# Attention scores of two heads in one three-bank PSUM tile, sink column and inverse denominators on GpSimd

## Chip, cores, metric

The kernel runs on one core of one Trainium2 chip. The metric is the device time of one execution in microseconds (us). A core has five engines with instruction streams of their own: TensorE (PE in the profile; its weight loads are listed as PEld), VectorE (DVE), ScalarE (ACT), GpSimd (POOL) and SyncE (SP), which issues most DMAs here. Each runs its instructions in order and waits on semaphores for the others. SBUF holds tiles of 128 partitions; PSUM, which matmuls write, has 8 banks of 512 f32 values a partition.

## What is computed

Two layers over 1024 latent and 256 context tokens. Layer 0 mixes with a chunked gMLP, layer 1 with windowed attention; a ConvGLU follows each. The change lies in the attention of layer 1: 16 query heads, 4 key/value heads, one softmax over the latent keys at a distance of at most 128, all 256 context keys and a sink logit of the head.

```
def softmax_with_sink(logits, sink):
    sink_col = jnp.broadcast_to(...)
    p = jax.nn.softmax(jnp.concatenate([logits, sink_col], axis=-1), axis=-1)
    return p[..., :-1]
...
    def one_block(args):
        j, qj = args
        kj = lax.dynamic_slice_in_dim(kp, j * BLOCK, band, axis=1)
        ...
        s_lat = jnp.einsum('bqhgd,bkhd->bhgqk', qj, kj).astype(jnp.float32) * scale
        s_lat = jnp.where(valid, s_lat, -jnp.inf)
        s_ctx = jnp.einsum('bqhgd,bkhd->bhgqk', qj, kc).astype(jnp.float32) * scale
        p = softmax_with_sink(jnp.concatenate([s_lat, s_ctx], axis=-1), sink)
```

## The kernel before

All matmuls run on float32 values split into a high and a low part in fp32r: `S.copy` rounds the high part on ACT and `V.tensor_sub` makes the rest on DVE.

Attention runs over `pairs` (L1849): query block `j` of 128 rows (8 of them), key/value head `g` (4), and a pair `pr` of its four query heads (2), so 64 pairs. Block 0 and block 7 see two latent key tiles, the others three, and all see two context tiles; a row of scores has NK = 512 or 640 columns, and NL of them are latent. The loop at the end of the kernel function (`for i in range(n_pairs + LC)`) issues for each `i`: `q_prep` (transposes of the next queries, one PSUM bank), `att_a` of pair i, `att_b` of pair i - 2, `att_c` of pair i - 3, then steps of the output projection `o_steps`.

- `att_a`: the scores, in two forms. Pairs 8 to NM - 1 = 23 are *merged*: each head has a two-bank tile `psA` of its own, six matmuls fill it (256, 256 and 128 columns, high and low keys), and one DVE instruction (`tensor_tensor_reduce`, `CUSTOM_DVE_ANT_0` in the profile, `ISA` in the order) adds the mask, writes the row to SBUF and takes its extreme with the sink logit. Other pairs are *split*: both heads' latent scores lie in one `psA` tile, a bank a head, both heads' context scores in one `psB` bank, and each head takes two such instructions, of NL and of 256 columns, the second starting from the first's extreme. Scores have their sign turned, so the maximum is a minimum here.
- `softmax`: from block 2 on (`es is None`) the sink logit stands as one more column behind the row. DVE copies it there (`V.tensor_copy`), ACT takes the exponential with its sum, DVE inverts the sums (`V.reciprocal`) and POOL scales the two rows. In blocks 0 and 1 POOL adds the sink's term and inverts as a power of -1 with the constant `mone`.
- `att_b`: the rows are transposed in 128 x 128 pieces into `psB` tiles, and ACT and DVE make high and low parts (`act`).
- `att_c`: products with the values into a `psB` tile; ACT copies one half, DVE adds the halves to the block's row tile. After a block's last pair the row tile is split and stored to `oscr` in DRAM, one DMA on ACT's queue and one on SP's.
- `o_steps`: the output projection for blocks 0 and 1, 2 and 3, 4 and 5, each in two halves of eight steps. Each step loads weights (`wh` from `woscr`) and rows (`oc` from `oscr`), and adds six 512-column matmuls to a `psA` tile that is held for a half. They start at i = 20, 36 and 52 (`sched`). At the end of a half ACT copies the tile to `acc`, in the step that follows the last matmuls. Blocks 6 and 7 are projected behind the loop (`last_o`).

PSUM is one pool `ps` for the whole kernel: `psA` twice two banks, `psB` four times one. Tiles come from rings: a tile of a tag takes the place of the one `bufs` allocations earlier and waits until that one is no longer used. The wait of a matmul for a reader of the same tile is set by the recording layer, and that layer also decides the order on each engine: it starts from the program's order and puts ahead what its own estimates take to be ready. So the order on an engine is a result, and a change of one operation can move others.

Names in the profile: `psB<-act,y` are the products with the values, `psB<-ident,tmp` and `psB<-ident,wl` the transposes of the two heads' rows, `psA<-big,tmp` and `psB<-big,tmp` the scores (`big` are the keys, `tmp` the queries), `psA<-wh,oc` the projection, `act<-psB,act` DVE's hi/lo difference of `att_b`, `sm` the small statistics. A row of a group has the line of a helper, L50, for all of them.

Of the kernel before, what the change touches and what calls it, by code (L numbers as in the profile page):

```python
# [32 lines left out]
def hybrid_kernel(  # L33
# [37 lines left out]
    open_pool("mix")  # L71
    ps = ctx.enter_context(tc.tile_pool(name="ps", bufs=1, space=bass.MemoryType.PSUM))
    dr = ctx.enter_context(tc.tile_pool(name="dr", bufs=1, space=bass.MemoryType.DRAM))
# [56 lines left out]
    def psA(shape=(P, 2, 512)):  # L130
        return ps.tile(list(shape), F32, name=nm("psA"), tag="psA", bufs=2)

    def psB(shape=(P, 512)):
        return ps.tile(list(shape), F32, name=nm("psB"), tag="psB", bufs=4)

# [43 lines left out]
    ones = ones_r.bitcast(F32)  # L179
    mhalf = const.tile([P, 1], F32, name="mhalf")  # L180
    G.memset(mhalf, -0.5)
    mone = const.tile([P, 2], F32, name="mone")
    G.memset(mone, -1.0)
# [639 lines left out]
    def gmlp(si, hb, tiles, gate, extra, between, pre_last, on_flip=None, head=None, order=(0, 1, 2, 3, 4), mod=None):  # L823
        st = const.tile([P, 5, 24], F32, name=nm("st"))
        if head:
# [28 lines left out]
        rs, nmr = t_sm(5), t_sm(5)  # L854
        mv = t_sm(10).rearrange("p (i n) -> p i n", i=5)
        for i in range(5):
# [960 lines left out]
    def after_b(bi, u):  # L1817
# [9 lines left out]
        if bi == 2:  # L1827
# [5 lines left out]
            if u == 2:  # L1833
                q_prep(0, 1)

    maskw = const.tile([P, 640], F32, name="mask")
    G.memset(maskw, 0.0)
# [4 lines left out]
                    pattern=[[-1, 384]], channel_multiplier=1)  # L1842
    NM = 24
    snk = const.tile([P, NH], F32, name="snk")
# [5 lines left out]
    HEAD = 2  # L1850

    def softmax(Pt, mx, es, dn, h0, NK):
        if es is None:
            for h in range(2):
                S.activation(Pt[h][:, 0:NK + 1], Pt[h][:, 0:NK + 1], AF.Exp, bias=mx[:, h:h + 1], scale=-1.0,
                             accum_out=dn[:, h:h + 1])
            V.reciprocal(dn, dn)
            for h in range(2):
                G.tensor_scalar(out=Pt[h][:, 0:NK], in0=Pt[h][:, 0:NK], scalar1=dn[:, h:h + 1], scalar2=0.0,
                                op0=ALU.mult, op1=ALU.add)  # L1860
            return
        G.tensor_tensor(out=es, in0=snk[:, h0:h0 + 2], in1=mx[:, 0:2], op=ALU.add)
        for h in range(2):
            S.activation(Pt[h][:, 0:NK], Pt[h][:, 0:NK], AF.Exp, bias=mx[:, h:h + 1], scale=-1.0,
                         accum_out=dn[:, h:h + 1])
        S.activation(es, es, AF.Exp)
        G.tensor_tensor(out=dn, in0=dn, in1=es, op=ALU.add)
        G.tensor_tensor(out=dn, in0=dn, in1=mone, op=ALU.pow)
        for h in range(2):
            G.tensor_scalar(out=Pt[h][:, 0:NK], in0=Pt[h][:, 0:NK], scalar1=dn[:, h:h + 1], scalar2=0.0,  # L1870
                            op0=ALU.mult, op1=ALU.add)

    def merged(j, g, pr):
        return 8 <= 8 * j + 2 * g + pr < NM

    def att_a(j, g, pr):
        k0, kts = geo[j]
# [4 lines left out]
        mx, es, dn = t_sm(4), t_sm(2) if j < 2 else None, t_sm(2)  # L1882
        Pt = [t_tmp((P, 648)), t_w("wl", F32, (P, 648))]
        if es is None:
            for h in range(2):
                V.tensor_copy(Pt[h][:, NK:NK + 1], nsnk[:, h0 + h:h0 + h + 1])
        if merged(j, g, pr):
            for h in range(2):
                lh = qs[:, 2 * pr + h, :]
                sl = psA()  # L1890
                for dst, c in ((sl[:, 0, 0:256], 1024), (sl[:, 0, 256:512], k0 * P), (sl[:, 1, 0:P], k0 * P + 256)):
# [3 lines left out]
                V.tensor_tensor_reduce(out=Pt[h][:, 0:NK], in0=sl.rearrange("p a b -> p (a b)")[:, 0:NK],  # L1895
                                       in1=maskw[:, 0:NK], scale=1.0,
                                       scalar=nsnk[:, h0 + h:h0 + h + 1], op0=ALU.add, op1=ALU.min,
                                       accum_out=mx[:, h:h + 1])
# [25 lines left out]
    def att_b(j, g, pr):  # L1924
# [3 lines left out]
        for a in range(0, nk, 2):  # L1928
            n = min(2, nk - a)
            pt = psB((P, 2, 2, P))  # L1930
            for b in range(n):
                for h in range(2):
                    T.transpose(out=pt[:, b, h, :], in_=Pt[h][:, (a + b) * P:(a + b + 1) * P], identity=ident)
            S.copy(PTh[:, a:a + n], pt[:, 0:n])
# [5 lines left out]
    def att_c(j, g, pr):  # L1940
        kts = geo[j][1]
        nk = len(kts)
        if merged(j, g, pr):
            kts = kts[-2:] + kts[:-2]
# [25 lines left out]
    def o_steps(tiles):  # L1970
# [34 lines left out]
        for i in range(nt):  # L2005
# [51 lines left out]
    while next(og, 1) is None:  # L2057
        tick()

    def last_o():  # L2060
# [20 lines left out]
    lat_ffn(1, 3, 5, halos, gate_of(1, 5), chain(last_o(), flushes(True)), ada_steps(1, 5, (0,), True))  # L2081
    stage_pool["guard"].__exit__(None, None, None)


# [40 lines left out]
```

## Time and profile before

| | us |
|---|---|
| median of three runs | 2849.98 (2846.95 to 2852.19) |
| the profiled execution | 2852.14 |
| its span, first to last instruction | 2850.4 |
| attention loop, pairs 20 to 63 | about 1883 to 2130 |
| mean granted TensorE clock | 0.99 |

The page gives busy times over the span, groups of instructions and the chain of work that ended last; the trace answers for any stretch. A group's row reads: line, engine, operation, names out<-in, shape, count | busy us, mean ns of one | idle time of the engine just before, with what ended it. A row of waits reads: engine, what it was to write, what it waited for: total us, times, longest. A row of the timeline: start, length, engine, operation, count, and in brackets the idle time before it. A matmul is listed with its full passage, so matmuls that follow each other overlap in the list; how far their starts lie apart is what each costs PE.

### The profile page before, as it was taken

Reading aid. Unit: us, or ns where it says so; the run is one execution under the profiler, and the core shown is the slowest. Engines: PE = TensorE matmul, PEld = TensorE weight load, DVE = VectorE, ACT = ScalarE, POOL = GpSimd, SP = SyncE. Lnnn points to the kernel's source line nnn. Section 1 sums busy time; section 2 is a strip of 40 time slices with the busy share of each in tenths; the row PEclk is TensorE's granted clock in tenths of the full one; section 3 lists DMA queues with packets and bytes.
Section 4 is the critical chain, followed back from the end, with each engine's and each line's share of the span. In section 5 each row is a group of like instructions: output and inputs, shape, how many; then the busy total and the mean of one; then the engine's idle time right before and its main releaser. Section 6 shows DMA issues by size and latency. Waiting matters only on the chain.

```text
span 2850.4 us, 40321 instructions
## 1 busy us (share of the span) xinstructions
PE 2735.4 (96%) x14570; PEld 2348.8 (82%) x14570; DVE 2218.6 (78%) x3466; ACT 1390.8 (49%) x2291; POOL 623.2 (22%) x806
## 2 busy tenths in 40 slices
PE   7999999999989999999999999899998999999998
PEld 5798887898879888888888788788887888888886
DVE  6567685687779898887786658898887788888776
ACT  4233243232367444455444545777876444445433
POOL 1064021260110122121000124543332122220000
PEclk9999999999999999999999999999999999999999
DMA  7785447554478345467845665347577355445753
GB/s 261 237 244 171 146 142 240 184 158 127 174 233 249 121 159 170 143 219 231 313 157 187 201 210 188 115 139 238 186 241 231 122 168 179 157 144 196 254 176 125
DMA packets 436335, 537.13 MB, mean 188 GB/s; under 512 B 20004, under 2 KB 300452, under 8 KB 436135
## 3 DMA queue, kind: packets, MB, share of 16 engines
q1 hardware_dynamic: 379575, 470.84, 51.5%
q10 hardware_dynamic: 55408, 59.52, 6.2%
q0 software_dynamic: 1152, 4.19, 0.4%
q8 instruction: 115, 1.88, 0.3%
q14 instruction: 85, 0.70, 0.1%
HBM read 414.40 MB, written 120.07 MB: 188 GB/s over the span
## 4 chain that ended last, share of the span: by engine, by line
PE 69%; DVE 12%; DMA 9%; ACT 4%; issue 4%; POOL 2%; SPq 1%; ACTq 0%; DVEq 0%; POOLq 0%
PE psB L50 52%; PE psA L50 17%; DVE row L50 3%; DMA raw<-in_ada_w_dram 3%; DVE wl L50 3%; DVE acc L50 1%; DVE tmp L50 1%; ACT wh L50 1%; DVE y L50 1%; ACT tmp L50 1%; DMA raw<-in_f_w_up_dram 1%; DMA xT<-row 1%; SPq L50 1%; POOL sm L50 1%; DVE act L50 1%
## 5 line engine op out<-in xcount | busy, mean ns | idle before, releaser
L50 PE MATMUL psB<-cmb,wh 128*128 128x512 f32 (+2 forms) x2584 | 750.5, 374 | 8.1 <-ACT row L50 5.6
L50 PEld LDWEIGHTS psB<-cmb,wh 128*128 128x128 f32 x2584 | 471.9, 188 | 99.2 <-ACT row L50 8.0
L50 PE MATMUL psB<-cmb,wl 128*128 128x512 f32 (+2 forms) x1292 | 482.9, 374 | 0.0
L50 ACT CAST wh<-raw 128x1024 fp32r<-128x1024 f32 (+1 forms) x313 | 265.2, 863 | 436.4 <-PE psB L50 173.6
L50 DVE TENSOR_TENSOR wl<-raw,wh 128x1024 fp32r<-128x1024 f32 (+1 forms) x313 | 308.9, 1002 | 97.2 <-ACT wh L50 95.5
L50 PEld LDWEIGHTS psB<-cmb,wl 128*128 128x128 f32 x1292 | 243.1, 188 | 43.6 <-DVE wl L50 0.2
L50 PE MATMUL psB<-wh,big 128*128 128x512 f32 x816 | 271.4, 399 | 4.0 <-ACT big L50 1.3
L50 ACT CAST wh<-row 128x1024 fp32r<-128x1024 f32 (+1 forms) x196 | 162.5, 834 | 189.9 <-DVE row L50 97.0
L50 PE MATMUL psB<-wh,act 128*128 128x512 f32 x640 | 200.2, 391 | 0.8 <-DVE tmp L50 0.8
L50 POOL TENSOR_TENSOR row<-raw,raw 128x512 f32<-128x512 f32 x44 | 73.2, 1664 | 572.2 <-DMA raw<-in_f_w_up_dram 516.6
L50 PE MATMUL psA<-big,wh 128*128 128x320 f32 x1024 | 194.4, 312 | 0.3 <-ACT row L50 0.3
L50 DVE TENSOR_TENSOR wl<-row,wh 128x1024 fp32r<-128x1024 f32 (+1 forms) x196 | 185.4, 949 | 11.8 <-ACT wh L50 11.8
L50 DVE SCALAR_TENSOR_TENSOR acc<-raw,ccols,acc 128x1024 f32<-128x1024 f32 x98 | 125.8, 1302 | 81.2 <-DMA raw<-in_ada_w_dram 81.1
L50 PEld LDWEIGHTS psB<-wh,big 128*128 128x128 f32 x816 | 154.7, 191 | 40.2 <-ACT big L50 2.4
L50 DVE SCALAR_TENSOR_TENSOR row<-row,cwcols,row 128x1024 f32<-128x1024 f32 (+2 forms) x142 | 150.8, 1062 | 39.2 <-ACT row L50 22.6
L50 ACT CAST ah<-raw 128x1024 fp32r<-128x1024 f32 x80 | 77.6, 974 | 202.2 <-PE psB L50 80.9
L50 POOL TENSOR_SCALAR row<-row,sm,sm 128x128 f32<-128x128 f32 x160 | 146.0, 926 | 114.0 <-DMA row<-vscr 63.3
L50 DVE TENSOR_TENSOR row<-row,row 128x512 f32<-128x512 f32 (+4 forms) x169 | 156.9, 932 | 17.3 <-DMA row<-actd 10.5
L50 PEld LDWEIGHTS psA<-big,wh 128*128 128x128 f32 x1024 | 160.9, 189 | 0.7 <-ACT row L50 0.5
L50 PE MATMUL psB<-wl,big 128*128 128x512 f32 x408 | 157.9, 397 | 0.6 <-DVE wl L50 0.6
L50 DVE TENSOR_TENSOR al<-raw,ah 128x1024 fp32r<-128x1024 f32 x80 | 90.3, 1128 | 71.4 <-ACT ah L50 71.1
L50 PE MATMUL psB<-row,wh 128*128 128x256 f32 x744 | 133.6, 283 | 9.5 <-ACT wh L50 7.5
(279 smaller groups left out, 6210.7 us busy)
## 6 DMA issues: line engine op xcount, KB each, us to landing
raw<-in_f_w_up_dram SPq DMA_DIRECT2D x121, 512.0 KB, 4.9
raw<-in_ada_w_dram SPq DMA_DIRECT2D x88, 512.0 KB, 4.4
raw<-in_a_w_in_dram SPq DMA_DIRECT2D x64, 512.0 KB, 4.6
wh<-woscr SPq DMA_DIRECT2D x48, 512.0 KB, 4.4
row<-actd SPq DMA_DIRECT2D x44, 512.0 KB, 5.3
actc<-row SPq DMA_DIRECT2D x44, 512.0 KB, 4.1
raw<-actc SPq DMA_DIRECT2D x40, 512.0 KB, 3.8
actd<-row SPq DMA_DIRECT2D x39, 512.0 KB, 2.6
```

Of the source, the lines that this page charges most:

```text
L50: ins = fn(*a, **kw)
```

## The change

- PSUM becomes three pools, one after the other. The first is as before and ends ahead of pair NM, now 20. The second has one score tile `psS` of three banks, one projection tile `psO` of two and three `psB`. The third, as the first, opens behind the loop. They are opened so that a tile waits only for the tiles whose place it takes.
- From pair 20 on all pairs are *joined*: both heads' scores lie in the one `psS`, head 0's row over banks 0 and 1 (its latent columns end where its context columns begin), head 1's over banks 1 and 2. Each head has four matmuls and one DVE instruction for the whole row. Head 0 has its latent columns first, head 1 its context columns, which `att_b`, `att_c` and the mask (256 columns longer) follow. Pairs 20 to 23 were merged before, 24 to 63 split.
- From pair 16 on the rows of a pair are allocated while the pair before is at its scores, and POOL copies the sink's column into them then.
- From block 2 on POOL inverts the denominators, as it did in blocks 0 and 1.
- `o_steps` copies the finished half to `acc` in the step of its last matmuls.
- Small constants share tiles (`powers`, and the statistics of the gMLP), which pays for the longer mask.

```
+    def psS():
+        return banks_pool["pool"].tile([P, 1536], F32, name=nm("psS"), tag="psS", bufs=1)
+
+    def psO():
+        return banks_pool["pool"].tile([P, 2, 512], F32, name=nm("psO"), tag="psO", bufs=1)
...
-    NM = 24
+    NM = 20
...
-            V.reciprocal(dn, dn)
+            G.tensor_tensor(out=dn, in0=dn, in1=mone, op=ALU.pow)
...
-        Pt = [t_tmp((P, 648)), t_w("wl", F32, (P, 648))]
-        if es is None:
+        Pt = rows_of.pop((j, g, pr), None) or [t_tmp((P, 648)), t_w("wl", F32, (P, 648))]
+        nxt = 8 * j + 2 * g + pr + 1
+        if 16 <= nxt < len(pairs):
+            nj, ng, npr = pairs[nxt]
+            rows_of[nj, ng, npr] = [t_tmp((P, 648)), t_w("wl", F32, (P, 648))]
+            nk = len(geo[nj][1]) * P
             for h in range(2):
-                V.tensor_copy(Pt[h][:, NK:NK + 1], nsnk[:, h0 + h:h0 + h + 1])
+                G.tensor_copy(rows_of[nj, ng, npr][h][:, nk:nk + 1],
+                              nsnk[:, 4 * ng + 2 * npr + h:4 * ng + 2 * npr + h + 1])
...
+        if joined(j, g, pr):
+            sl = psS()
+            for h in range(2):
+                lh = qs[:, 2 * pr + h, :]
+                local, o = (512 - NL, 512 - NL) if h == 0 and j < 7 else (512 * h + 512, 512 * h + 256)
+                context = 512 if h == 0 and j < 7 else 512 * h + 256
+                for c, k, n in ((local, k0 * P, NL), (context, 1024, 256)):
+                    T.matmul(sl[:, c:c + n], lh, KH[g][:, k:k + n], start=True, stop=False)
+                    T.matmul(sl[:, c:c + n], lh, KL[g][:, k:k + n], start=False, stop=True)
+                m = 256 if h == 0 and j < 7 else 0
+                V.tensor_tensor_reduce(out=Pt[h][:, 0:NK], in0=sl[:, o:o + NK], in1=maskw[:, m:m + NK], scale=1.0,
+                                       scalar=nsnk[:, h0 + h:h0 + h + 1], op0=ALU.add, op1=ALU.min,
+                                       accum_out=mx[:, h:h + 1])
             softmax(Pt, mx, es, dn, h0, NK)
...
-            pacc = psA()
+            pacc = psO()
...
+                if k == KD - 1:
+                    for i in range(nt):
+                        S.copy(ys[i][:, h * 512:(h + 1) * 512], pacc[:, i, :])
                 yield
-            for i in range(nt):
-                S.copy(ys[i][:, h * 512:(h + 1) * 512], pacc[:, i, :])
...
+        if i == NM:
+            open_banks("ps2", reuse_waits="tile")
+            banks_pool["small"] = 3
...
+    open_banks("ps3", reuse_waits="tile")
```

What it moves, at three places. First TensorE, the scores of one pair in the middle of the loop, before: `psA_18250` holds both heads' latent and `psB_18251` both heads' context scores, and what stands in brackets are the semaphores that a matmul waits for.

```order
L50 MATMUL psA_18250<-big_15654,tmp_18090 128x384
L50 MATMUL psA_18250<-big_15655,tmp_18090 128x384
L50 MATMUL psB_18251<-big_15654,tmp_18090 128x256 [waits DVE_49]
L50 MATMUL psB_18251<-big_15655,tmp_18090 128x256
L50 MATMUL psA_18250<-big_15654,tmp_18090 128x384
L50 MATMUL psA_18250<-big_15655,tmp_18090 128x384
L50 MATMUL psB_18251<-big_15654,tmp_18090 128x256
L50 MATMUL psB_18251<-big_15655,tmp_18090 128x256
```

Now, the second head of a pair there; its tile `psS_18123` had the first head's four matmuls nine transposes earlier.

```order
L50 MATMUL psB_18155<-ident,tmp_17911 128x128 [waits DVE_49,Activation_49]
L50 MATMUL psS_18123<-big_15651,tmp_18048 128x384 [waits DVE_49]
L50 MATMUL psS_18123<-big_15652,tmp_18048 128x384
L50 MATMUL psS_18123<-big_15651,tmp_18048 128x256
L50 MATMUL psS_18123<-big_15652,tmp_18048 128x256
L50 MATMUL psB_18155<-ident,wl_17912 128x128
L50 MATMUL psO_17739<-wh_18035,oc_17969 128x512 [waits DMAHW7_49]
```

The eight matmuls that stood together are two groups of four, with transposes, projection or value products between; the first matmul of each group waits for DVE.

Second VectorE, one pair of the loop before: the two heads' rows are `tmp_19100` and `wl_19101`.

```order
L50 ISA tmp_19100,sm_19098<-psA_19104,mask,nsnk 128x384
L50 ISA sm_19098 128x1
L50 ISA wl_19101,sm_19098<-psA_19104,mask,nsnk 128x384
L50 ISA sm_19098 128x1
L50 ISA tmp_19100,sm_19098<-psB_19105,mask,sm_19098 128x256
L50 ISA sm_19098 128x1
L50 ISA wl_19101,sm_19098<-psB_19105,mask,sm_19098 128x256
L50 ISA sm_19098 128x1
L50 TENSOR_TENSOR act_19124<-psB_19125,act_19123 128x512
L50 TENSOR_TENSOR act_19124<-psB_19132,act_19123 128x512
L50 TENSOR_TENSOR act_19124<-psB_19139,act_19123 128x256
L50 RECIPROCAL sm_19099<-sm_19099 128x2
```

Now, one pair with the rows `tmp_17911` and `wl_17912`.

```order
L50 ISA tmp_17911,sm_17977<-psS_17983,mask,nsnk 128x640
L50 ISA sm_17977 128x1
L50 TENSOR_TENSOR act_18000<-psB_18001,act_17999 128x512
L50 ISA wl_17912,sm_17977<-psS_17983,mask,nsnk 128x640
L50 ISA sm_17977 128x1
L50 TENSOR_TENSOR act_18000<-psB_18008,act_17999 128x512
L50 TENSOR_TENSOR act_18000<-psB_18015,act_17999 128x256
L50 TENSOR_TENSOR row_17642<-psB_18020,tmp_18031 64x128 x2
```

Four row instructions have become two, the reciprocal and the column copies are gone, and a difference of another pair now stands between the two heads.

Third TensorE again, ahead of the first projection matmul of blocks 4 and 5 (`oc_19694` and `oc_19592` are their first rows from DRAM), before:

```order
L50 MATMUL psB_19675<-act_19576,y_14763 128x256
L50 MATMUL psB_19675<-act_19577,y_14763 128x256
L50 MATMUL psB_19702<-ident,row_19246 128x128 x4
L50 MATMUL psB_19716<-big_15735,tmp_19549 128x256
L50 MATMUL psB_19716<-big_15736,tmp_19549 128x256
L50 MATMUL psB_19716<-big_15735,tmp_19549 128x256
L50 MATMUL psB_19716<-big_15736,tmp_19549 128x256
L50 MATMUL psA_19770<-wh_19692,oc_19694 128x512 x2
```

and now:

```order
L50 MATMUL psB_19568<-ident,tmp_19314 128x128
L50 MATMUL psB_19568<-ident,wl_19315 128x128
L50 MATMUL psO_19665<-wh_19590,oc_19592 128x512 x2
L50 MATMUL psS_19536<-big_15732,tmp_19455 128x384
L50 MATMUL psS_19536<-big_15733,tmp_19455 128x384
```

Before, the value products of two pairs, two query transposes and the scores of three pairs stood between the last product of block 5 and this matmul; now the products of one pair and the scores of one and a half do, and the next scores follow it.

More of the change, by code (lines that the diff above doesn't have):

```diff
@@ L71, in hybrid_kernel, with open_banks @@
     open_pool("mix")
-    ps = ctx.enter_context(tc.tile_pool(name="ps", bufs=1, space=bass.MemoryType.PSUM))
+    banks_pool = {}
+    def open_banks(name, **kw):
+        if banks_pool:
+            banks_pool.pop("guard").__exit__(None, None, None)
+        banks_pool["guard"] = tc.tile_pool(name=name, bufs=1, space=bass.MemoryType.PSUM, **kw)
+        banks_pool["pool"] = banks_pool["guard"].__enter__()
+        banks_pool["small"] = 4
+    open_banks("ps")
     dr = ctx.enter_context(tc.tile_pool(name="dr", bufs=1, space=bass.MemoryType.DRAM))
@@ L130, in psA @@
     def psA(shape=(P, 2, 512)):
-        return ps.tile(list(shape), F32, name=nm("psA"), tag="psA", bufs=2)
+        return banks_pool["pool"].tile(list(shape), F32, name=nm("psA"), tag="psA", bufs=2)
+    def psS():
+        return banks_pool["pool"].tile([P, 1536], F32, name=nm("psS"), tag="psS", bufs=1)
+    def psO():
+        return banks_pool["pool"].tile([P, 2, 512], F32, name=nm("psO"), tag="psO", bufs=1)
     def psB(shape=(P, 512)):
-        return ps.tile(list(shape), F32, name=nm("psB"), tag="psB", bufs=4)
+        return banks_pool["pool"].tile(list(shape), F32, name=nm("psB"), tag="psB", bufs=banks_pool["small"])
     def wsplit(dview, a):
@@ L179, in hybrid_kernel @@
     ones = ones_r.bitcast(F32)
-    mhalf = const.tile([P, 1], F32, name="mhalf")
+    powers = const.tile([P, 3], F32, name="powers")
+    mhalf, mone = powers[:, 0:1], powers[:, 1:3]
     G.memset(mhalf, -0.5)
-    mone = const.tile([P, 2], F32, name="mone")
     G.memset(mone, -1.0)
@@ L823, in gmlp @@
     def gmlp(si, hb, tiles, gate, extra, between, pre_last, on_flip=None, head=None, order=(0, 1, 2, 3, 4), mod=None):
-        st = const.tile([P, 5, 24], F32, name=nm("st"))
+        stats = const.tile([P, 184], F32, name=nm("st"), tag="st")
+        st = stats[:, 0:120].rearrange("p (i n) -> p i n", i=5)
         if head:
@@ L854, in gmlp @@
         rs, nmr = t_sm(5), t_sm(5)
-        mv = t_sm(10).rearrange("p (i n) -> p i n", i=5)
+        mv = stats[:, 120:130].rearrange("p (i n) -> p i n", i=5)
         for i in range(5):
@@ L1834, in after_b @@
                 q_prep(0, 1)
-    maskw = const.tile([P, 640], F32, name="mask")
+    maskw = const.tile([P, 896], F32, name="mask")
     G.memset(maskw, 0.0)
@@ L1850, in hybrid_kernel @@
     HEAD = 2
+    rows_of = {}
     def softmax(Pt, mx, es, dn, h0, NK):
@@ L1874, in merged, with joined @@
         return 8 <= 8 * j + 2 * g + pr < NM
+    def joined(j, g, pr):
+        return 8 * j + 2 * g + pr >= NM
     def att_a(j, g, pr):
@@ L1896, in att_a @@
                                        in1=maskw[:, 0:NK], scale=1.0,
+                                       scalar=nsnk[:, h0 + h:h0 + h + 1], op0=ALU.add, op1=ALU.min,
+                                       accum_out=mx[:, h:h + 1])
+            softmax(Pt, mx, es, dn, h0, NK)
+            at[(j, g, pr)] = Pt
+            return
+        if joined(j, g, pr):
[9 more added lines that the diff above has]
+                V.tensor_tensor_reduce(out=Pt[h][:, 0:NK], in0=sl[:, o:o + NK], in1=maskw[:, m:m + NK], scale=1.0,
                                        scalar=nsnk[:, h0 + h:h0 + h + 1], op0=ALU.add, op1=ALU.min,
@@ L1932, in att_b @@
                 for h in range(2):
-                    T.transpose(out=pt[:, b, h, :], in_=Pt[h][:, (a + b) * P:(a + b + 1) * P], identity=ident)
+                    c = (a + b + 3) % 5 if h == 0 and nk == 5 and joined(j, g, pr) else a + b
+                    T.transpose(out=pt[:, b, h, :], in_=Pt[h][:, c * P:(c + 1) * P], identity=ident)
             S.copy(PTh[:, a:a + n], pt[:, 0:n])
@@ L1942, in att_c @@
         nk = len(kts)
-        if merged(j, g, pr):
+        if merged(j, g, pr) or joined(j, g, pr):
             kts = kts[-2:] + kts[:-2]
@@ L2082, in hybrid_kernel @@
     stage_pool["guard"].__exit__(None, None, None)
+    banks_pool["guard"].__exit__(None, None, None)
 _INS = ['x', 'c', 'ctx', 'c_ctx', 'ada_w', 'ada_b', 'norm_g', 'a_w_in', 'a_ln_g', 'a_ln_b', 'a_w_s', 'a_b_s',
```

## Prediction

> **What bounds the kernel now.** I read the page first. TensorE (PE) is busy 96% of the span and stands for most of the chain that ended last, so the change pays only where PE stands still.
>
> ```profile
> span 2850.4 us, 40321 instructions
> PE 2735.4 (96%) x14570; PEld 2348.8 (82%) x14570; DVE 2218.6 (78%) x3466; ACT 1390.8 (49%) x2291; POOL 623.2 (22%) x806
> PE 69%; DVE 12%; DMA 9%; ACT 4%; issue 4%; POOL 2%; SPq 1%; ACTq 0%; DVEq 0%; POOLq 0%
> ```
>
> Then the view by stretches, for the part that the change touches: pairs 20 to 63 of the attention loop run from about 1883 to 2130 us, and the loop's end lies behind it. Columns: stretch, length, then busy time of PE, weight loads (PEld), DVE, ACT and POOL.
>
> ```profile
> 1883.00:1940.00 57.00, 54.59 (x376) 48.38 (x375) 53.73 (x169) 42.22 (x99) 23.82 (x27) 1.00 0.75 251
> 1940.00:2130.00 190.00, 180.03 (x1232) 161.51 (x1231) 162.70 (x566) 143.07 (x328) 63.26 (x92) 0.98 0.65 215
> 1883.00:2130.00 247.00, 234.62 (x1606) 209.89 (x1605) 216.43 (x734) 185.28 (x427) 87.07 (x118) 0.99 0.67 223
> ```
>
> PE stands idle 247.00 - 234.62 = 12.4 us there. DVE is 94% busy in the first 57 us and 86% in the rest. Who is waited for, in the view of waits of this stretch, first by PE, then by its weight loads:
>
> ```profile
> PE psB L50 <- DVE sm L50: 4.8, 5, 1.6
> PE psA L50 <- DMA oc<-oscr: 2.6, 1, 2.6
> PE psB L50 <- DVE act L50: 1.9, 3, 0.8
> PE psA L50 <- DVE sm L50: 1.3, 3, 0.5
> ...
> PEld psB L50 <- DVE sm L50: 9.3, 18, 1.8
> PEld psA L50 <- DVE sm L50: 4.0, 8, 0.9
> ```
>
> DVE is waited for 4.8 + 1.9 + 1.3 = 8.0 us by PE and 9.3 + 4.0 = 13.3 us by the weight loads, which lie partly under running matmuls. So 8 us is what a lighter DVE gains if all of it is seen, and some 13 is the upper bound. The DMA takes 2.6.
>
> **What DVE is spared.** Its groups of this stretch, each form by itself:
>
> ```profile
> L50 DVE CUSTOM_DVE_ANT_0 wl<-psA,mask,nsnk 128x384 f32<-128x384 f32 x32 | 19.6, 614 | 0.0
> L50 DVE CUSTOM_DVE_ANT_0 wl<-psB,mask,sm 128x256 f32<-128x256 f32 x40 | 19.2, 480 | 0.0
> L50 DVE CUSTOM_DVE_ANT_0 tmp<-psA,mask,nsnk 128x640 f32<-128x640 f32 x4 | 3.5, 874 | 0.0
> L50 DVE RECIPROCAL sm<-sm 128x2 f32<-128x2 f32 x43 | 7.0, 164 | 8.3 <-ACT wl L50 7.9
> L50 DVE COPY tmp<-nsnk 128x1 f32<-128x1 f32 x44 | 6.5, 148 | 0.9
> L50 DVE COPY wl<-nsnk 128x1 f32<-128x1 f32 x42 | 5.4, 143 | 0.8 <-PE psB L50 0.8
> L50 DVE TENSOR_TENSOR act<-psB,act 128x512 fp32r<-128x512 f32 x86 | 56.1, 684 | 2.1 <-ACT act L50 1.9
> ```
>
> A split head costs 614 + 480 = 1094 ns, a joined one 874: 0.22 saved, 64 heads, 14 us. The 16 heads of block 7 have 512 columns, which no row shows; two of 480 become one of something between 614 and 874, say 0.74: 3.5 us. Copies go (two a pair, 6.5 + 5.4 us) and reciprocals (7.0). That is 36 us of 216 busy, of which about a third lay under the neighbouring instruction (in DVE's rows below a copy of 0.16 is followed 0.07 later), so some 24 us of DVE's time. Pairs 20 to 23 were merged, with one instruction a head already, and lose only copies and reciprocal, as do pairs 16 to 19 before the stretch. **Worth on PE:** between 0 and 13 us; I take **-6**, nearer to the 8 that PE itself shows, because the hi/lo differences (684 ns each, the last row), for which PE's value products wait, stay as they are.
>
> **What is added: two hand-overs a pair.** In the rows of the order, head 1's four score matmuls now stand behind a wait for DVE, which is head 0's maximum, and the next pair's head 0 waits for head 1's. With one tile there are 2 x 44 - 1 = 87 such turns PE, DVE, PE. Before, a split pair made all eight matmuls in a row and waited once, with about 4 us of other matmuls between. The price is in pair 20 of before, a merged pair for which a second tile was not free. PE's rows, then DVE's:
>
> ```profile
> 1884.52 0.91 PE L50 MATMUL psA<-big,tmp 128*128 128x256 f32 x6 [0.43 <-DVE sm L50]
> 1885.32 1.43 PE L50 MATMUL psB<-act,y 128*128 128x256 f32 x10
> ```
>
> ```profile
> 1883.51 0.16 DVE L50 COPY tmp<-nsnk 128x1 f32<-128x1 f32 x1
> 1883.58 0.87 DVE L50 CUSTOM_DVE_ANT_0 tmp<-psA,mask,nsnk 128x640 f32<-128x640 f32 x1
> ...
> 1885.46 0.88 DVE L50 CUSTOM_DVE_ANT_0 wl<-psA,mask,nsnk 128x640 f32<-128x640 f32 x1
> ```
>
> The second maximum starts 0.03 us after the end of its matmuls (1884.52 + 0.91 = 1885.43) and lasts 0.88; the first ended at 1884.45 and PE went on at 1884.52, 0.07 later. With the last matmul's own 0.2 to 0.3 us, a turn takes some 1.25 us from that matmul's start, so PE needs about 1.15 us of other work to cover it, and more when DVE is still at something else. How much work the new order has in between I summed over its rows: transposes start 0.11 us apart, 256-column matmuls 0.12, 512-column ones 0.23, by rows like these.
>
> ```profile
> 2046.04 0.27 PE L50 MATMUL psB<-ident,wl 128*128 128x128 f32 x1
> 2046.15 0.27 PE L50 MATMUL psB<-ident,tmp 128*128 128x128 f32 x1
> ...
> 2058.01 1.39 PE L50 MATMUL psB<-act,y 128*128 128x256 f32 x10
> ...
> 2021.13 2.01 PE L50 MATMUL psA<-wh,oc 128*128 128x512 f32 x8
> ```
>
> The mean is 1.8 us, but 30 of the 87 have under 1.15 (nine transposes are 0.98) and 47 under 1.7. The shortfalls sum to 6 us for a need of 1.15, 14 for 1.4 and 26 for 1.7. With a lighter DVE I take 1.25: about 9. From it go 1.3 that PE waited at this place before and about 1.5 that falls into waits for DMA: **+6**, between +3 and +22.
>
> By the Trainium skill ("PSUM — Partial Sum Buffer", section "PSUM bank collisions raise a hardware error"), PE and DVE are to be kept apart by bank, not by address. Of head 1's matmuls that would hold back the two 256-column ones, whose bank head 0's maximum reads, and free the two 384-column ones in the third bank; with 0.35 us more work under 44 turns the sum would be some 4 us lower. The order's wait stands ahead of all four.
>
> **The output projection.** Its first matmul of a block pair waits for attention rows that go out to DRAM and come back. The rows of the second such place:
>
> ```profile
> 1962.73 1.42 PE L50 MATMUL psB<-act,y 128*128 128x256 f32 x10
> ...
> 1977.71 1.40 PE L50 MATMUL psA<-wh,oc 128*128 128x512 f32 x3 [2.64 <-DMA oc<-oscr]
> ...
> 1968.36 0.53 SPq L50 DMA_DIRECT2D oscr<-row  x1
> 1973.94 0.37 SPq L50 DMA_DIRECT2D oc<-oscr  x1
> ```
>
> The block's last product ends at about 1964.0, the load is issued at 1973.9 (the store took 5.6) and PE goes on at 1977.7, 13.7 us in all. By counts of rows times spacing, the order before has some 8.7, 7.6 and 9.2 us of PE work between last product and first projection matmul at the three places, and the new one 6.2, 6.8 and 6.6: 6 us less cover. Only the second place shows a wait for DMA, so most of that was covered by nothing but DVE's lateness: **+2**, between 0 and +6. Copying the projection's result one step earlier, and its own tile, I cost at 0: three or more us of other work stand between two halves.
>
> **Pool.** The inverse as a power is in this trace for the first 16 pairs:
>
> ```profile
> L50 POOL TENSOR_TENSOR sm<-sm,mone 128x2 f32<-128x2 f32 x16 | 11.4, 710 | 1.1
> L50 POOL TENSOR_SCALAR tmp<-tmp,sm 128x640 f32<-128x640 f32 x48 | 39.3, 819 | 136.4 <-DVE sm L50 88.3 <-PE psA L50 24.5 <-DVE tmp L50 16.5
> ```
>
> It takes 710 ns for DVE's 164, so the two scalings behind it start about 0.5 us later, and two copies of one column stand ahead of it in Pool's queue. Pool idled 136 us before those scalings, so it has room, and the transposes that need the scaled rows come a pair later. **+0.5**, between 0 and +3. If that cover went, each of 44 pairs would pay up to 0.5. The change of PSUM pools at pair 20 and behind the loop: **+0.5**, 0 to +2. Wider mask, shared constants: nothing; they are written once, at the start, and no row of the loop waits for Pool's constants.
>
> **Sum:** -6 + 6 + 2 + 0.5 + 0.5 = **+3 us** on the profiled execution's 2852.1 (span 2850.4 and 1.7 around it). That execution lies 2.2 us above the median of the runs, 2849.98; the same step from the median gives **2853**.
>
> **Rivals.** *DVE is the real bound* (chance 0.30). For it: 94% busy in the first 57 us. Against it: the long second part, where PE waits little. Then nearly all 13 us come back, the turns cost their minimum (+3), the projection nothing: -9, some **2841**. *The hand-overs take over* (0.30), slower: DVE, in order, is still at the hi/lo differences (0.68 us each) when the scores are done, and a turn needs 1.7 us. Then +22, +4 for the projection, -6 for DVE, -3 for overlap: +17, **2867**. It decides from a need of about 1.35 us, where the shortfalls outgrow the relief by more than 6. *Nothing that can be measured* (0.40), with my sum inside: both effects are of one size. That the change does not do as it says can be left out: the order shows the maxima halved and the reciprocals gone.
>
> A measurement here tells 0.2%, 5.7 us, from no change. Faster by more: 0.30; within: 0.40; slower by more: 0.30. The range takes in both rivals with a little beyond: 2838 to 2868.
>
> **What would show it.** Right: DVE's busy time in the loop down by 30 us or more; PE's waits for DVE's difference shorter; new waits of PE, named DVE, ahead of the score matmuls, 5 to 10 us in total; loop length within 6 us of 247. The first rival: PE idle under 8 us. The second: waits at the scores over 15 us. Wrong altogether: an end of the loop that moves by more than 20 us, or times that change before 1836 us, where order and work are the same.

## The result and the profile after

The changed kernel takes 2871.89 us (median of 4 runs, 2867.45 to 2873.34), the kernel before 2850.51 in the same set: 1.0075 times, interval 1.006 to 1.009. It is slower by 21 us; 2853 was forecast, with 2838 to 2868 as the range.

The page of the changed kernel, span and engines, and its chain by engine:

```profile
span 2870.9 us, 40099 instructions
PE 2742.6 (96%) x14554; PEld 2351.1 (82%) x14554; DVE 2197.6 (77%) x3162; ACT 1394.6 (49%) x2291; POOL 668.8 (23%) x950
PE 67%; DVE 12%; DMA 10%; ACT 4%; issue 4%; POOL 2%; SPq 1%; ACTq 0%; DVEq 0%; POOLq 0%
```

The page alone misleads: DVE has 21 us less to do, and PE, with 16 matmuls fewer, is busy 7 us longer. The view by stretches says where. I took both traces from the start of the last matmul of pair 15's value products to that of pair 63's, so that the same 48 pairs stand in both; before first, then after (columns: stretch, length, busy time of PE, PEld, DVE, ACT, POOL, granted clock of PE, DMA share, GB/s):

```profile
1874.39:2139.33 264.94, 251.16 (x1726) 224.99 (x1725) 232.27 (x772) 201.40 (x459) 91.59 (x124) 0.99 0.66 218
```

```profile
1870.94:2155.00 284.06, 258.74 (x1708) 228.26 (x1707) 212.75 (x478) 204.36 (x461) 140.06 (x257) 0.97 0.62 205
```

The loop is 19.1 us longer, nearly the whole loss. PE's idle time grew from 13.8 to 25.3 us (length less busy). The other 7.6 us are busy time, for 18 matmuls fewer. In part PE ran slower, at a mean clock of 0.97 and not 0.99: the clock stands at half for 17.1 us of the changed loop and for 6.8 of the loop before, PE is busy for 15.3 and 6.8 us of that, and half of it is lost, 7.7 and 3.4 us. That makes some 4 of the 7.6; the rest was not taken apart.

Whom PE waited for in these two stretches, by the view of waits (us in total, times, longest). Before:

```profile
PE psB L50 <- DVE sm L50: 4.8, 5, 1.6
PE psA L50 <- DMA oc<-oscr: 2.6, 1, 2.6
PE psB L50 <- DVE act L50: 2.4, 5, 0.8
PE psA L50 <- DVE sm L50: 2.3, 4, 1.0
```

After:

```profile
PE psB L50 <- DVE act L50: 7.9, 9, 1.4
PE psO L50 <- DMA oc<-oscr: 7.4, 2, 4.7
PE psS L50 <- DVE sm L50: 3.9, 6, 0.9
PE psS L50 <- DVE row L50: 3.2, 1, 3.2
```

The `sm` rows are the maxima. The waits for them fell, from 7.1 to 3.9 us, hand-overs included. What grew is the wait for `act`, DVE's hi/lo differences (2.4 to 7.9), the projection's wait for DMA (2.6 to 7.4), and a single wait of 3.2 us at the change of pools. The rows ahead of that one, PE's:

```profile
1874.56 1.39 PE L50 MATMUL psB<-act,y 128*128 128x256 f32 x10
1879.13 0.83 PE L50 MATMUL psS<-big,tmp 128*128 128x384 f32 x4 [3.18 <-DVE row L50]
```

and DVE's at the same time:

```profile
1874.46 0.88 DVE L50 CUSTOM_DVE_ANT_0 wl<-psA,mask,nsnk 128x640 f32<-128x640 f32 x1
...
1876.88 1.62 DVE L50 TENSOR_TENSOR act<-psB,act 128x512 fp32r<-128x512 f32 x3 [0.39 <-ACT act L50]
1878.42 0.57 DVE L50 TENSOR_TENSOR row<-psB,tmp 64x128 f32<-64x128 f32 x2
```

The last maximum was done at 1875.34, but the new score tile lies on the banks of older value products, whose sums (`row`) DVE finished at 1878.99. By their order in the trace these are the ten matmuls at 1874.56, pair 16's (and not pair 17's, as an expectation below has it). The groups that the change made, by form:

```profile
L50 DVE CUSTOM_DVE_ANT_0 wl<-psS,mask,nsnk 128x640 f32<-128x640 f32 x36 | 31.7, 881 | 15.5 <-PE psS L50 13.8 <-PE psB L50 1.0 <-POOL wl L50 0.4
L50 POOL TENSOR_TENSOR sm<-sm,powers 128x2 f32<-128x2 f32 x44 | 31.2, 709 | 86.4 <-ACT wl L50 80.2 <-DVE row L50 3.5 <-DVE act L50 2.7
L50 DVE CUSTOM_DVE_ANT_0 wl<-psS,mask,nsnk 128x512 f32<-128x512 f32 x8 | 6.0, 744 | 0.6 <-PE psS L50 0.6
```

These are the durations that the prediction put in (874, 710, 740): the instructions cost what was said. What it did not count is the PSUM itself: three banks for the scores and two for the projection leave three small buffers (`psB`), where there were four.

### The profile page after: what moved, and what is told of

Read it like the earlier page. It is cut to its first block, busy times and chain, and to the rows that moved or that the text cites. A ratio compares the mean times of both kernels' runs of the same rounds, so it can differ in the third digit from the quotient of the medians.

```text
span 2870.9 us, 40099 instructions
## 1 busy us (share of the span) xinstructions
PE 2742.6 (96%) x14554; PEld 2351.1 (82%) x14554; DVE 2197.6 (77%) x3162; ACT 1394.6 (49%) x2291; POOL 668.8 (23%) x950
## 4 chain that ended last, share of the span: by engine, by line
PE 67%; DVE 12%; DMA 10%; ACT 4%; issue 4%; POOL 2%; SPq 1%; ACTq 0%; DVEq 0%; POOLq 0%
PE psB L50 50%; PE psA L50 13%; DVE row L50 3%; DMA raw<-in_ada_w_dram 3%; DVE wl L50 3%; PE psO L50 2%; PE psS L50 2%; DVE tmp L50 1%; DVE acc L50 1%; ACT tmp L50 1%; ACT wh L50 1%; DMA raw<-in_f_w_up_dram 1%; DMA xT<-row 1%; DVE y L50 1%; POOL sm L50 1%
## 5 line engine op out<-in xcount | busy, mean ns | idle before, releaser
L50 POOL TENSOR_TENSOR sm<-sm,powers 128x2 f32<-128x2 f32 (+2 forms) x86 | 66.2, 770 | 640.8 <-DVE sm L50 547.8
```

What stands on the lines that cost most here:

```text
L50: ins = fn(*a, **kw)
```

## Experiments

Each kernel was timed beside the kernel before, whose median in these sets was 2850.3 to 2851.8. "Loop" is the stretch of the 48 pairs as above, "clock" the mean granted clock in it, both from one profiled execution of each.

| kernel | median us | ratio to before, interval | loop us | clock |
|---|---|---|---|---|
| before | 2850.5 | 1 | 264.9 | 0.99 |
| changed | 2871.9 | 1.0075, 1.0060 to 1.0090 | 284.1 | 0.97 |
| before + Pool edits | 2852.3 | 1.0006, 0.9997 to 1.0015 | 264.8 | 0.99 |
| changed, DVE's copies and inverse back | 2870.7 | 1.0075, 1.0062 to 1.0089 | 277.9 | 0.98 |
| before + change of pools, four buffers | 2855.8 | 1.0019, 1.0008 to 1.0030 | 269.6 | 0.97 |
| before + change of pools, three buffers | 2871.7 | 1.0078, 1.0065 to 1.0090 | 285.9 | 0.98 |
| before, projection later | 2850.0 | 0.9997, 0.9988 to 1.0005 | 267.1 | 0.99 |
| changed, projection later | 2860.9 | 1.0037, 1.0024 to 1.0050 | 271.7 | 0.99 |
| changed, score tile on other banks | 2868.1 | 1.0060, 1.0045 to 1.0075 | 280.4 | 0.98 |
| changed, one transpose moved | 2866.1 | 1.0052, 1.0036 to 1.0067 | 278.6 | 0.98 |
| changed, these three together | 2860.4 | 1.0030, 1.0021 to 1.0040 | 274.4 | 0.98 |
| changed, quarters, three buffers | 2871.0 | 1.0067, 1.0046 to 1.0088 | 286.5 | 0.97 |
| changed, quarters, four buffers | 2863.2 | 1.0044, 1.0028 to 1.0060 | 276.9 | 0.98 |
| the same, projection later ("repaired") | 2850.7 | 1.0001, 0.9990 to 1.0012 | 268.5 | 0.99 |
| repaired, score tile on other banks | 2852.1 | 1.0003, 0.9995 to 1.0012 | 266.2 | 1.00 |
| repaired, DVE's copies and inverse back | 2853.2 | 1.0012, 1.0003 to 1.0020 | 267.6 | 0.99 |
| repaired, two maxima a head | 2865.0 | 1.0054, 1.0041 to 1.0068 | 279.8 | 0.98 |

One caution on loop lengths and waits: the kernel with one transpose moved has the changed kernel's order on PE up to the loop's end, and yet its loop was 5.5 us shorter in its one profiled execution (its waits for DMA 4.2 and not 7.4 us). Differences of that size are read from the medians.

**The Pool edits alone.** Into the kernel before, nothing else changed:

```diff
-            V.reciprocal(dn, dn)
+            G.tensor_tensor(out=dn, in0=dn, in1=mone, op=ALU.pow)
...
+                G.tensor_copy(rows_of[nj, ng, npr][h][:, nk:nk + 1],
+                              nsnk[:, 4 * ng + 2 * npr + h:4 * ng + 2 * npr + h + 1])
```

> The kernel before with the two Pool edits alone (sink's column one pair ahead, inverse of the denominators as a power), its four small PSUM buffers and its score tiles kept. Theory A, the relief of DVE is worth something as long as the PSUM buffers stay as they were: PE's waits for DVE's maxima at the context scores, 4.8 us, shrink; 3 to 6 us faster than before, some 2846. Rival C, the inverse on Pool (0.77 us) is too late for the transposes: 5 us or more slower than before, with PE or its weight loads waiting for Pool. Rival B, the hand-overs over the single score tile are the whole loss: it says nothing of this part alone, and allows anything from -6 to 0.

Its loop, by stretches, and the two largest waits of PE in it:

```profile
1871.81:2136.64 264.83, 249.83 (x1726) 225.00 (x1724) 221.77 (x637) 200.81 (x460) 142.29 (x257) 0.99 0.66 218
```

```profile
PE psB L50 <- DVE sm L50: 5.4, 6, 1.5
PE psB L50 <- DVE act L50: 4.4, 6, 1.6
```

DVE has 10.5 us less to do than in the loop before, and PE waits for it no less. The relief from this part is worth nothing that can be measured, and the longer inverse on Pool costs nothing: rival C falls, and so does theory A's 3 to 6 us.

**The score tile alone.** The changed kernel with both edits taken back:

```diff
-            G.tensor_tensor(out=dn, in0=dn, in1=mone, op=ALU.pow)
+            V.reciprocal(dn, dn)
...
+                V.tensor_copy(Pt[h][:, NK:NK + 1], nsnk[:, h0 + h:h0 + h + 1])
```

> The changed kernel with the sink's copies and the inverse back on DVE: the score tile of three banks, its pools and three small buffers alone. Theory A (the loss is in the PSUM layout: three small buffers, the change of pools, less cover for the projection) and rival B (the hand-overs): as slow as the changed kernel or up to 5 us slower, 2870 to 2877, since DVE has some 19 us more to do and each hand-over waits a little longer. Rival C (Pool's longer chain is the loss): 10 us or more faster than the changed kernel, below 2862.

As slow as the changed kernel. The loss is in the PSUM layout and what hangs on it, the order of the instructions included. Its trace spreads the waits otherwise, 2.8 us for `act` and 4.9 for DMA where the changed kernel has 7.9 and 7.4, so the rows of one trace don't price a single wait.

**The change of pools, with three small buffers and with four, in the kernel before.** Score matmuls, maxima and DVE's work stay; the second differs from the first in one number.

```diff
+        if i == 20:
+            open_banks("ps2", reuse_waits="tile")
+            banks_pool["small"] = 3
...
+    open_banks("ps3", reuse_waits="tile")
```

> The kernel before with three small PSUM buffers in place of four from pair 20 to the loop's end, one bank left unused; two score matmul tiles, two maxima a head and DVE's copies as before. Theory A: the missing buffer costs 5 to 12 us (2855 to 2863), and PE's waits for DVE's hi/lo difference, 1.9 us in the loop before, rise to 6 or more. Here a pair takes five small tiles, not four, so it is rather an upper bound of the price in the changed kernel. Rival B, only the hand-overs count: within 3 us of before.

> The kernel before with the change of PSUM pools at pair 20 and behind the loop, all four small buffers and both score tiles kept. Theory A: only the waits at the two changes, 2 to 5 us: 2853 to 2856, so that of the run with three buffers 15 us and more belong to the missing buffer. Rival: the change of pools is what cost that run its time: 2865 or more.

PE's waits in the loop, with three buffers:

```profile
PE psB L50 <- DVE act L50: 9.9, 12, 2.2
PE psB L50 <- DVE row L50: 4.9, 8, 1.4
```

and with four:

```profile
PE psA L50 <- DVE row L50: 3.4, 1, 3.4
PE psB L50 <- DVE act L50: 2.4, 5, 0.8
```

This is the clearest pair of the study: one small buffer fewer costs 15.9 us (2871.7 less 2855.8, from two sets; 16.8 by the ratios to the kernel before), more than the 5 to 12 expected, and it shows as waits for the readers of the small buffers, the hi/lo differences and the rows' sums. The change of pools by itself costs 5.1 us (2 to 9 by the interval); the one wait of 3.4 is what its trace shows of it. Since a pair of the kernel before takes five small tiles and one of the changed kernel four, the buffer's price there should be lower.

**A fourth buffer in the changed kernel.** The projection accumulates quarters of 256 columns, so that two tiles' accumulators fit in one bank; the attention rows are loaded four times.

```diff
-        return banks_pool["pool"].tile([P, 2, 512], F32, name=nm("psO"), tag="psO", bufs=1)
+        return banks_pool["pool"].tile([P, 2, 256], F32, name=nm("psO"), tag="psO", bufs=1)
...
-            banks_pool["small"] = 3
+            banks_pool["small"] = 4
```

> The changed kernel with the output projection in quarters of 256 columns: its accumulators take one PSUM bank in place of two, and the bank goes to a fourth small buffer. The attention rows are loaded four times in place of twice, matmuls of 512 columns become two of 256. To be read against the next run, which has the quarters but three small buffers. Theory (the missing fourth buffer is a main part of the loss): 5 to 10 us faster than the next run, and PE's waits for DVE's hi/lo difference, 7.9 us in the changed kernel, under 3. Rival (the hand-overs over the score tile are the limit, the buffer is not): within 2 us of the next run.

> The projection in quarters as in the run before it, with three small buffers as in the changed kernel and one bank unused. It prices the quarters themselves (twice the loads of attention rows, shorter matmuls): 0 to 6 us slower than the changed kernel, 2872 to 2878; both theories say the same of it.

The loops, three buffers first:

```profile
1872.89:2159.38 286.49, 261.71 (x1997) 246.15 (x1995) 212.76 (x475) 202.83 (x472) 141.24 (x257) 0.97 0.74 244
```

```profile
1873.56:2150.43 276.87, 254.99 (x1996) 242.63 (x1995) 212.89 (x475) 202.74 (x472) 141.04 (x257) 0.98 0.76 253
```

The quarters cost nothing, the buffer is worth 7.8 us by the medians, as expected (their intervals overlap: 1.0046 to 1.0088 and 1.0028 to 1.0060) and 9.6 in the loop. The second half of the expectation failed: the named wait for `act` did not fall (3.9 us with three, 4.6 with four). The waits for maxima at the scores did, from 6.1 to 2.2. The two orders differ as well: summed as in the prediction, the shortfalls of the 87 hand-overs for a need of 1.15 us are 11.8 us with three buffers and 6.7 with four. So the price of the missing buffer doesn't stand at the waits for that buffer alone: the order is another one too, and the two were not told apart.

**The projection later.** One line of the schedule, first in the changed kernel, then in the kernel before:

```diff
-    sched = ((20, 36, 0, 19), (36, 52, 19, 19), (52, 66, 38, 19))
+    sched = ((21, 37, 0, 19), (37, 53, 19, 19), (53, 66, 38, 19))
```

> The changed kernel with the output projection's steps of the first two block pairs one pair later, so that the first matmuls of the second and third have 9.3 and 7.9 us of PE work ahead (6.8 and 6.6 in the changed kernel). Theory A: PE's waits for the DMA of attention rows, 7.4 us there, fall by 3 to 4, and so does the time: 2866 to 2869. Rival: the wait is only handed on to another place (the third block has fewer pairs to spread its steps over): within 2 us of the changed kernel, 2870 to 2874.

> The kernel before with the projection's steps one pair later in its first two block pairs (14.7, 12.7 and 12.3 us of PE work ahead of the first matmuls, 8.7, 7.6 and 9.2 before). If a later projection is a gain of its own, it takes away the 2.6 us wait for DMA here: 2848 or less. If its gain of 11 us belongs to the changed kernel's lack of cover and buffers: within 2 us of 2851, or slower, since the third block pair has fewer pairs left.

In the changed kernel it brings 11 us, three times what was expected, in the kernel before nothing (there the DMA's wait of 2.6 us is gone, and the waits for `act` are 5.9 us in place of 2.4). The changed kernel's loop with it, and PE's waits there:

```profile
1869.23:2140.94 271.71, 254.25 (x1708) 224.10 (x1707) 213.37 (x477) 204.27 (x461) 143.66 (x257) 0.99 0.65 213
```

```profile
PE psO L50 <- DMA oc<-oscr: 4.9, 2, 3.2
PE psS L50 <- DVE row L50: 3.2, 1, 3.2
...
PE psB L50 <- DVE act L50: 1.9, 4, 0.6
```

Between the two traces, whose loops differ by 12.4 us, the DMA's waits fell by 2.5, the waits for `act` by 6.0 (7.9 to 1.9), and PE's busy time by 4.5 for the same 1708 matmuls, at a clock of 0.99. The moved steps changed the order around them; that PE now comes to the transposes when the buffers are free is a reading of these rows. Which of the reordered rows does it was not tried apart.

**Two single places.** At the change of pools, the tiles laid out in another order (the order of the instructions is the same on every engine):

```diff
             banks_pool["small"] = 3
+            psB()
+            psO()
```

> The changed kernel with the three kinds of PSUM tiles laid out in another order at pair 20, so that the score tile takes the banks of pair 19's score tiles (free at 1875.3 us in the changed kernel's trace) and not those of pair 17's value products. The order of the instructions is the same on every engine. Theory: PE's single wait of 3.2 us for DVE's row ahead of pair 20's scores goes; 3 us faster than the changed kernel, about 2869. Rival: DVE and Pool are behind at that place anyway and the wait comes back at the next transposes or hand-overs: within 1 us, 2871 to 2873.

In its rows the wait at the scores is gone and a similar one stands at the next transposes:

```profile
1874.33 0.75 PE L50 MATMUL psS<-big,tmp 128*128 128x384 f32 x4
1877.67 1.30 PE L50 MATMUL psB<-ident,tmp 128*128 128x128 f32 x5 [2.58 <-DVE row L50]
```

So the rival is right about the mechanism, although the median is 3.8 us lower (the intervals overlap). Behind the loop, one transpose stood 14 rows too early in the changed kernel:

```profile
2159.87 0.40 PE L50 MATMUL psA<-wl,row 128*128 128x512 f32 x1
2164.83 0.48 PE L50 MATMUL psB<-ident,acc 128*128 128x128 f32 x1 [4.56 <-POOL acc L50]
```

```diff
-            T.transpose(out=pq[k // 4][:, k % 4, :], in_=xn[:, k * P:(k + 1) * P], identity=ident)
+            ins = T.transpose(out=pq[k // 4][:, k % 4, :], in_=xn[:, k * P:(k + 1) * P], identity=ident)
+            if stage == 3 and t == 4:
+                tc.keep_in_program_order(ins)
```

> The changed kernel with one transpose moved: the first of tile 4's transposes behind the loop stands with its seven fellows behind the projection matmuls, not 14 rows ahead of them. Theory: PE's wait of 4.6 us for Pool there goes; 4 to 5 us faster than the changed kernel, about 2867. Rival: the projection matmuls behind it would have waited for their weights or for ACT's and DVE's last rows as the kernel before did there (4.2 us in two waits): under 1.5 us gained, 2870 to 2872.

It brings 5.8 us by the medians (the intervals overlap); the wait is gone, and from pair 63's products to the last projection matmul behind the loop it takes 31.1 us in place of 34.9. Since the kernel before takes 35.0 there, with other waits, this was a gain to be had, not a part of the loss. All three single edits together:

> The changed kernel with three edits together: the projection's steps one pair later, the score tile in pair 19's banks at the change of pools, and the first transpose behind the loop with its fellows. If the three losses are single places that add up (11 + 3 + 4.5 of the changed kernel's 2872): 2853, the time before. If they hide each other: 2858 to 2861, no better than the later projection alone. If the single score tile's hand-overs are the real limit: not below 2858.

They don't add up: no better than the projection later alone, in the size that was expected if they hide each other. That they do was not shown, for the three places lie far apart: with all three edits the stretch behind the loop is 3.1 us shorter than with the later projection alone (31.3 and 34.4), and the loop 2.7 longer, one execution each.

**The repaired kernel.** Quarters with four small buffers, the projection one pair later, the transpose kept with its fellows:

> The changed kernel with the projection in quarters, four small buffers, the projection's steps one pair later and the transpose behind the loop with its fellows. Theory (buffer and projection's cover are the loss, the hand-overs cost about 7): 2850 to 2857, level with the kernel before at best. Rival (hand-overs are the floor): not below the later projection alone, 2860 or more.

```profile
1868.02:2136.49 268.47, 253.63 (x1996) 241.54 (x1995) 209.63 (x474) 204.69 (x472) 140.65 (x257) 0.99 0.78 259
```

```profile
PE psS L50 <- DVE row L50: 3.2, 1, 3.2
PE psS L50 <- DVE sm L50: 3.0, 7, 1.1
...
PE psB L50 <- DVE act L50: 1.4, 4, 0.5
```

It is level with the kernel before, on the single score tile with its 87 hand-overs. The quarters alone and the later projection in the kernel before brought nothing, so most of what came back here is what the change had lost, and the hand-overs, taken together with the relief, are not the loss. Two reservations: the moved transpose is in this kernel too, though the stretch behind the loop is no shorter for it (33.0 us, against 32.8 in the quarters with four buffers, without that edit). And that stretch is 2.0 us shorter than in the kernel before, the loop 3.5 us longer. The four medians make a square: 2871.9 as changed (2871.0 with the quarters), 2863.2 with the buffer, 2860.9 with the projection later, 2850.7 with both. The buffer brings 8 to 10 us, the later projection 11 to 12.5 (the last corner with the transpose moved as well).

**What is left of relief and hand-overs**, on the repaired kernel. The score tile on pair 19's banks, as above:

> The kernel of p9_q4later (four small buffers, projection in quarters and one pair later, transpose behind the loop with its fellows) with the score tile in the banks of pair 19's score tiles; the order of the instructions is the same. If the wait at the change of pools (3.2 us there) is on the path: 2847 to 2849, 2 to 3 us faster than that kernel and than the kernel before. Rival, as in p7_three: the wait comes back at the next transposes: within 1 us of 2850.7.

Nothing to be measured (1.4 us slower, the intervals overlap), as the rival said. DVE's copies and inverse back:

> The kernel of p9_q4later with the sink's copies and the inverse on DVE again. Theory (the relief of DVE is real where the buffers suffice; this part is some 19 us of its busy time, about half): 3 to 6 us slower than p9_q4later, 2854 to 2857. Rival (DVE's free time is worth nothing, PE waits for the length of the chain of one pair and not for DVE's throughput, as in p1_pool_only): within 1.5 us of p9_q4later.

2.5 us slower, between the two expectations, and the intervals overlap (1.0003 to 1.0020 against 0.9990 to 1.0012): open. Two maxima a head on the one tile:

```diff
+                for a, b, first, to in ((0, NL, nsnk[:, h0 + h:h0 + h + 1], mx[:, 2 + h:3 + h]),
+                                        (NL, NK, mx[:, 2 + h:3 + h], mx[:, h:h + 1])):
```

> The kernel of p9_q4later with two maxima a head in place of one, on the same score tile: each of the 87 hand-overs takes 0.2 us longer and DVE does 88 instructions and some 17 us more. By the prediction's shortfalls (6 us for a need of 1.15, 14 for 1.4): 6 to 10 us slower, 2857 to 2861, with PE's excess time at the score matmuls, 18 us in p9_q4later, at 24 or more. Rival (the hand-overs are covered and cost nothing): within 2 us of p9_q4later.

14 us slower, more than expected, and not where expected:

```profile
PE psS L50 <- DVE sm L50: 4.8, 11, 0.8
PE psO L50 <- ACT acc L50: 3.6, 2, 2.8
...
PE psB L50 <- POOL wl L50: 1.8, 2, 1.3
PE psB L50 <- POOL tmp L50: 1.6, 3, 1.0
```

The waits at the scores rose by 1.8 us only. The order had put more work between the hand-overs (fewer than ten of 87 with under 1.15 us, nearly thirty in the repaired kernel). The waits that are new or longer name ACT's copy of the projection and POOL's rows, which come behind the maxima. The longer maximum costs, but by which link was not taken apart.

No version beats the kernel before by anything measurable.

## Why the prediction was wrong

**The step that failed** is "the change of PSUM pools at pair 20 and behind the loop: +0.5". It counted the hand-over of banks and not what the new pool holds: small buffers for transposes and value products go from four to three. No term of the sum stands for that, although only one of a pair's five small tiles, the context scores, leaves these buffers. The missing buffer is worth 7.8 us in the changed kernel with quarters, 15.9 in the kernel before. Even the part that was counted was mis-sized: one wait of 3.2 us at pair 20, 5.1 us by the timed pair, against an upper end of 2.

**The projection's first matmul: +2, between 0 and +6.** This is the second term that failed: the mechanism was right, the size was not. With less cover the DMA waits grew by 4.8 us, inside the range (by 1.6 in another execution of the same order). But the place is worth 11 us to the changed kernel, where PE's waits for `act` and the time at half clock (17.1 to 6.8 us) fall along with it; in the kernel before, the same step later is worth nothing.

**Relief -6, hand-overs +6.** Their sum was about right, as far as the runs show: the waits for maxima, 7.1 us before, are 3.9 after, and the repaired kernel, which has both, is level. Neither term was measured alone, so each of them may still be off. By the named waits the hand-overs came out low: 3.9 us at the scores, where 5 to 10 were to show. The run with two maxima warns that their price can stand elsewhere. Half of the relief, copies and inverse, brought nothing where it was tried alone; taking it out of the repaired kernel stays open (2.5 us); the rest was not tried alone. DVE's busy time in the loop fell by 19.5 us, not by 30 or more, near the 24 that the prediction's own working gave.

**Pool +0.5, copying earlier 0.** The first was right: 709 ns for the inverse as said, and the kernel without the Pool edits is as slow. The second was not tried alone; no wait of PE for that copy stands in the changed loop's list.

**The rival "the hand-overs take over", 2867,** is near in time and wrong in cause: over 15 us of waits at the scores were its mark, and 3.9 with the 3.2 at the change of pools were found.

**The marks.** The loop's length was to stay within 6 us and grew by 19.1; PE's waits for DVE's difference were to be shorter and grew from 2.4 to 7.9. The loop's end moved by 15.7 us, under the 20 named, because this execution was 3.5 us ahead at pair 15; PE's order is the same up to about 1861 us, and the kernel with one transpose moved, of the changed kernel's order there, comes to that point 6.3 us later, so that is scatter between executions. The same seems to hold for the 4.8 us that come after the loop's end (span 20.5 longer): the kernel before with the Pool edits was 2.7 us ahead at that point and ends level.

**What the prediction had no term for** is the clock. Some 4 of the loop's 19 us are matmuls at half rate behind the waits.

## What to carry to other kernels

When tiles are merged in PSUM, write down the banks before and after, and price every buffer that another kind of tile loses, even where the merged tiles leave that kind: here one of four was worth 8 to 16 us, more than the 6 that the merging and the Pool edits were forecast to save. Where an order is laid out ahead of the run, a lost buffer or a lost stretch of cover is not paid only at its own wait; ask it with a pair of kernels that differ in that one number. And when a profile shows less work on one engine and the same time, try the relief alone first: a shorter queue on an engine that is waited for through a chain may be worth nothing.

## What the hardware showed

PE's clock fell to half after far shorter gaps than I would have looked for. In the changed kernel, between the scores of pair 41 and the products of pair 37, PE waits 0.76 us up to 2011.5 and 1.35 up to 2014.1; the clock in stretches of one microsecond (the third number from the right):

```profile
2012.00:2013.00 1.00, 0.77 (x7) 0.53 (x5) 0.59 (x2) 0.99 (x4) 0.11 (x1) 1.00 1.03 239
2013.00:2014.00 1.00, 0.00 (x0) 0.00 (x0) 1.00 (x4) 0.98 (x2) 0.00 (x0) 0.86 0.87 303
2014.00:2015.00 1.00, 0.88 (x4) 0.91 (x5) 0.89 (x2) 0.44 (x3) 0.15 (x2) 0.50 1.01 372
2015.00:2016.00 1.00, 1.00 (x6) 1.00 (x6) 0.42 (x1) 0.26 (x1) 0.90 (x3) 0.50 1.13 415
2016.00:2017.00 1.00, 1.00 (x7) 1.00 (x6) 0.00 (x0) 0.04 (x1) 1.00 (x2) 0.50 0.99 377
2017.00:2018.00 1.00, 0.96 (x8) 0.72 (x6) 0.57 (x2) 0.76 (x2) 1.00 (x4) 0.94 1.09 333
```

```profile
2011.48 0.85 PE L50 MATMUL psS<-big,tmp 128*128 128x384 f32 x4 [0.76 <-DVE sm L50]
...
2014.12 0.45 PE L50 MATMUL psB<-ident,tmp 128*128 128x128 f32 x1 [1.35 <-DVE act L50]
2014.36 0.42 PE L50 MATMUL psB<-ident,wl 128*128 128x128 f32 x1
2014.44 2.48 PE L50 MATMUL psB<-act,y 128*128 128x256 f32 x10
```

The ten products of a pair take 2.48 us there and 1.39 at full clock (the row at 1874.56 above). Two waits of 2.1 us in all cost some 1.5 us more in slow matmuls (half of the 3.0 us in which PE is busy at half clock, second row below), so a wait's price is not its length. The Trainium skill ("TensorE: Matmul & The Clock Gate", "Part 1: The HAM clock gate") says that PE goes to half rate after an idle window of some 3.4 us and comes back after as long a stretch of work. The way back agrees: half rate for a little over 3 us. The way down does not: no gap here was longer than 1.4 us. The measurement decides, and two short waits close together are enough. The section "A second HAM failure mode: psum-queue depth-cycling" of the same page of the Trainium skill is nearer to it: there, short idle times between groups of matmuls that cycle through PSUM banks make the clock swing. The trace agrees in kind; the first of the two waits is one for the score tile's banks, the second one for a small buffer.

The traces show what the drop goes by. In the loops the clock stands at half for 3.41 us or twice that, and the stretch just before this drop is one in which PE is busy for half of the time:

```profile
2010.31:2013.72 3.41, 1.70 (x11) 1.14 (x9) 2.77 (x7) 3.11 (x8) 1.70 (x3) 1.00 0.89 250
2013.72:2017.13 3.41, 3.01 (x14) 3.04 (x15) 1.60 (x4) 1.16 (x4) 2.18 (x4) 0.50 1.02 379
```

I divided 320 us around the loop of each of the 17 profiled kernels into such stretches, in step with the changes of the clock. It fell 37 times, always after a stretch with PE busy for at most half of it (the highest 50.1%); of the 1531 stretches at full clock after which it stayed, three had PE busy for less than half (44 to 49%). So here it is the idle time summed over 3.41 us that goes with the drop, not the longest wait.
